# Sample-token products of several weight pairs run together, in a hybrid decoder step on one core

## The chip, the cores and the metric

The kernel runs on one core of one Trainium2 chip, as one launch. The metric is the device time of that launch in microseconds (us). The engines are named as the profile names them: PE (TensorE's matmuls) and PEld (its weight loads), DVE (VectorE), ACT (ScalarE), POOL (GpSimd) and SP (SyncE, which here issues most DMAs).

## The reference, cut to what matters

One layer of a decoder step for 1024 prompt tokens and 32 sample tokens (8 sequences of 4). Every token is normalised and modulated to `h`, `h` is projected by one wide matrix, an mLSTM branch and a windowed attention branch use the parts, two gates weigh the two output projections, and a last matrix ends the layer.

```python
def layer(x, c, C0, n0, m0, k_past, v_past, ...):
    h, gate = adaln_in(x, c, w_ada, b_ada, g_norm)
    (mq, mk, mv, mi, mf, mo, mz, aq, ak, av, az, gm, ga) = split_in(h @ w_in)
    y_m, C, n, m = mlstm_branch(mq, mk, mv, mi, mf, mo, mz, C0, n0, m0, ...)
    ...
    y_a = o.astype(x.dtype) * jax.nn.silu(az)
    u = jax.nn.sigmoid(gm) * (y_m @ w_mo) + jax.nn.sigmoid(ga) * (y_a @ w_ao)
    x = x + gate * (u @ w_o)
```

Both the prompt tokens and the sample tokens go through `h @ w_in`, `y_a @ w_ao` and so on, with the same weights.

## The kernel before, in words

**Products.** Each float32 operand is split into a high and a low part (`wh`, `wl` for weights; names ending in `h` and `l` for activations), and a product is made of three matmuls. ACT makes the high part by a cast, DVE the low part by a subtraction.

**Pairs.** 36 blocks of 128 output columns of `w_in` are done two at a time, as 18 pairs (class `Pair`, numbered 0 to 17): 0 to 3 belong to the mLSTM heads (`head_in`), 4 to 11 are the gates `ga` and `gm` (`gate`), 12 and 13 `az` (`query_gate`), 14 to 17 `mo` and `mz` (`head_gate`). A pair's prompt tokens are computed by seven block products in place of eight (a Strassen-like scheme): products 1 to 7 use sums and differences of four weight tiles, which DVE makes in place (`first_sums`, `split`). `block_products` runs them in the order 5, 6, 2, 7, then product 1 of the next pair, then 3, 4. Each product is 12 matmuls of 128x512 into the PSUM banks `bx`, `bw`, `by`, `bz`. Four pairs of `w_ao` (class `AttPair`, generator `att_products`, banks `ax`, `aw`, `ay`, `az`) follow the same way with half as many matmuls in a product; their operands `ya...` are made from `yr` tiles by ACT, DVE and POOL.

**Samples.** The 32 sample columns of a pair are not in these products. `samples` multiplies the raw weights with the sample tokens (`c32`) in a run of its own: 16 float32 matmuls (8 in the attention output) that use 32 columns of the array each, so that four work side by side, into a PSUM tile `smp` (`smpa`), which ACT copies to `smps`. One pair later `samples_end` transposes `smps` on PE into `smpo` (`halves_sum`, through `tr`), DVE adds the halves, and the pair's own function applies the gate to the samples (`gts`). In `block_products` both stand behind product 2 of pair n: first the transpose of pair n, then the sample run of pair n+1. In `att_products` they stand at the same place.

**Weights.** A pair's four raw tiles are loaded by SP (`nxt.load()` at product 5 of the pair before, two products ahead of the sample run) into a ring of nine tiles (`raw_tile`). Most other transient data, DMA targets included, live in 50 tiles of 128x512 (`ht`, tag "half").

**Order.** PE's order is the program's: `in_order` chains every matmul behind the last. On the other engines a scheduler orders the instructions when the kernel is built; `no_sync` gives it an order without a wait. `side` is a clock that the build keeps (`side.now`), by which other streams of work (the heads, the output weights) are set between the matmuls. SP issues its DMAs in one order, each waits at the head of the queue.

Of the kernel before, what the change touches and what calls it, by code (L numbers as in the profile page):

```python
# [15 lines left out]
ALU = mybir.AluOpType  # L16
# [8 lines left out]
NS = NB * NT  # L25
# [159 lines left out]
def body(tc, a):  # L185
    nc = tc.nc
    with ExitStack() as ctx:
# [35 lines left out]
        class Ordered:  # L223
            def __init__(self, eng, name):
                self.eng, self.name, self.on, self.late, self.before = eng, name, True, False, None

            def __getattr__(self, op):
                f = getattr(self.eng, op)

                def call(*args, **kw):  # L230
                    ins = f(*args, **kw)  # L231
                    i = getattr(ins, "ins", ins)
                    if self.on:
                        in_order(ins, self.name)
                    elif self.late and self.before is not None:
                        no_sync(i, [self.before])
                    self.before = i
                    return ins
                return call

        @contextmanager
        def not_before(*engs):
            for e in engs:
                e.late = True
            yield
            for e in engs:
                e.late = False

        V, S, G = Ordered(nc.vector, "V"), Ordered(nc.scalar, "S"), Ordered(nc.gpsimd, "G")
# [305 lines left out]
        def split_weights(raws, name, eng):  # L555
            parts = [split4(raw, f"{name}_{i}", eng) for i, raw in enumerate(raws)]
            return tuple((lambda k, w=w: w[k // 4][:, k % 4]) for w in zip(*parts))
# [3 lines left out]
        def piece(w, rh, rl, kn, name, p, evac):  # L561
            wh, wl = w
            c0, n = PIECES[p]
            banks.append(banks.pop(0))
            acc = banks[-1]([128, 384], f"g_{name}{p}")
            o = acc[:, :n]
            for k in range(kn):
                mm(o, wh(k), rh(k, c0, n), start=(k == 0), stop=False)
                mm(o, wh(k), rl(k, c0, n), start=False, stop=False)
                mm(o, wl(k), rh(k, c0, n), start=False, stop=(k == kn - 1))  # L570
                if k < kn - 1:
                    side.tick()
            evac(p, acc, c0, n)
            side.tick()

        hs = {}

# [834 lines left out]

        def halves_sum(sums):
            o, t = pb([128, 2, 2, NS], "smpo"), sums[:, 0:2 * NS].rearrange("p (c s) -> p c s", c=2)
            tr(o.rearrange("p c h s -> p (c h s)"), sums, ident)
            V.tensor_reduce(t, o.rearrange("p c h s -> p c s h"), op=ALU.add, axis=AX.X)
            return t

        class Pair:
# [5 lines left out]

            def load(self):
                for c, n in enumerate(self.names):
                    for kh in range(2):
                        t = self.raw[c, kh] = raw_tile(f"wr_{n[0]}{n[1]}_{kh}")
                        dma(t, a["w1"][JOBS[n]][:, 4 * kh:4 * kh + 4])  # L1430

            def samples(self):
                acc = pb([128, 128], "smp")
                for k in range(4):
                    for j in range(4):
                        mm(acc[32 * j:32 * j + 32], c32[:, 4 * (j % 2) + k], self.raw[j // 2, j % 2][:, k],
                           start=(k == 0), stop=(k == 3), share=4)
                self.sums = ht([128, 128], "smps")
                S.copy(self.sums, acc)

            def samples_end(self):
                self.kind.samples(self, halves_sum(self.sums))

            def first_sums(self, behind=None):
                self.raw["s1"] = raw_tile("ws1")
                V.tensor_tensor(self.raw["s1"], self.raw[1, 0], self.raw[1, 1], op=ALU.add)
                if behind is not None:
                    no_sync(V.before, [behind])
                V.tensor_tensor(self.raw[1, 0], self.raw[0, 0], self.raw[1, 0], op=ALU.subtract)
                V.tensor_tensor(self.raw[0, 0], self.raw["s1"], self.raw[0, 0], op=ALU.subtract)  # L1450

            def split(self, i):
                r = self.raw
                t = {1: r[0, 0], 2: r[0, 1], 3: r[0, 1], 4: r[1, 1], 5: r.get("s1"), 6: r[0, 0], 7: r[1, 0]}[i]
                self.w[i] = split4(t, f"p{self.name}_{i}_")
                if i == 2:
                    V.tensor_tensor(r[0, 1], r[0, 1], r[0, 0], op=ALU.subtract)
# [88 lines left out]
        class head_gate:  # L1546
# [14 lines left out]
            def samples(self, o):  # L1561
# [6 lines left out]
                store(ymD[h][:, SEQ:T], t[:, 0])  # L1568

        def block_products(jobs, hook):  # L1570
            flat = [(0, 1)]
# [26 lines left out]
            for j, (n, i) in enumerate(flat):  # L1598
                job_ = jobs[n]
                nxt = jobs[n + 1] if n + 1 < len(jobs) else None  # L1600
                hook(n, i)
                if i == 3 and not nxt:
                    job_.samples_end()
                job_.kind.ahead(job_, i)
                if i == (5 if n else 6) and nxt:
                    nxt.load()
                split_ahead(j + 2)
# [17 lines left out]
                elif i == 2:  # L1625
                    job_.done(0, 0, X)
                    behind = job_.weighted if job_.kind is query_gate else None
                elif i == 5:
                    p5 = ht([128, 512], "p5")
                    S.copy(p5, Z)  # L1630
                elif i == 3:
                    job_.done(0, 1, p5, W)
                elif i == 4:
                    job_.done(1, 0, Y)
                if i == (7 if n else 5):
                    job_.done(1, 1, p5, Y)
                if i == (2 if n else 7) and nxt:
                    job_.samples_end()
                    nxt.samples()
                    side.free["b"] = side.now + HOLD["b"]  # L1640
# [3 lines left out]
                if i == 7 and nxt and nxt.kind not in (head_in, gate):  # L1644
                    nxt.first_sums(behind)
                if j == 0 or (i == 3 and nxt):
# [49 lines left out]

        class AttPair:
            HOMES = {1: ("A", 0), 5: ("A", 2), 6: ("B", 0), 2: ("B", 2), 7: ("C", 0), 3: ("C", 2), 4: ("D", 0)}

            def __init__(self, i):  # L1700
                self.i, self.w, self.g = i, {}, {}

            def load(self):
                self.raw = [raw_tile(f"wr_ao{2 * self.i + c}") for c in range(2)]
                for c in range(2):
# [10 lines left out]

            def samples(self):
                acc = pb([128, 128], "smpa")
                for k in range(2):
                    for j in range(4):  # L1720
                        mm(acc[32 * j:32 * j + 32], c32[:, 2 * (j % 2) + k], self.raw[j // 2][:, 2 * (j % 2) + k],
                           start=(k == 0), stop=(k == 1), share=4)
                self.sums = ht([128, 128], "smps")
                S.copy(self.sums, acc)

            def samples_end(self):
                us = ut[self.i % 2][:, self.i // 2 * 2:self.i // 2 * 2 + 2, SEQ:T]
                V.scalar_tensor_tensor(us, self.ts, 1.0, halves_sum(self.sums), op0=ALU.add, op1=ALU.mult)

            def first_sums(self):  # L1730
                (r0, r1), s = self.raw, raw_tile("ws1")
                V.tensor_tensor(s[:, 0:2], r1[:, 0:2], r1[:, 2:4], op=ALU.add)
                V.tensor_tensor(r1[:, 0:2], r0[:, 0:2], r1[:, 0:2], op=ALU.subtract)
# [3 lines left out]
            def split(self, i):  # L1737
# [5 lines left out]
                hi, lo = self.w[i] = [x[:, o:o + 2] for x in self.g[home]]  # L1743
                S.copy(hi, t)
                V.tensor_tensor(lo, t, hi.bitcast(F32), op=ALU.subtract)
# [9 lines left out]
        def att_products():  # L1755
            jobs = [AttPair(i) for i in range(4)]
            flat = [(0, 1)]
# [17 lines left out]
            jobs[0].split(1)  # L1775
            jobs[0].samples()
            jobs[0].first_sums()
# [4 lines left out]
            for j, (n, i) in enumerate(flat):  # L1782
                job_ = jobs[n]
                nxt = jobs[n + 1] if n < 3 else None
                if i == 1 and nxt:
                    nxt.load()
                if i == 6:
                    if nxt:
                        nxt.gates()
                    if n in (0, 1, 3):  # L1790
# [282 lines left out]
        def hook(n, i):  # L2073
# [19 lines left out]
        work = block_products(pairs, hook)  # L2093
        att = att_products()
        side.add("g", ada_gate())
# [350 lines left out]
```

## Time and profile before

| | |
|---|---|
| median of 3 runs | 816.8 us (816.77 to 817.11) |
| the profiled execution's own time | 816.58 us |
| its span, first to last instruction | 814.8 us |
| mean granted TensorE clock | 0.995 |
| busy, share of the span | PE 98%, PEld 82%, DVE 74%, ACT 52%, POOL 10% |

Matmul records overlap since the engine is pipelined, so what a matmul costs is read here from start to start. In a timeline row the first number is the start in us from the span's start, the second the length, then engine, line, operation, output and inputs, shapes, and in brackets the idle time ahead with what ended it. An instruction of float32 in the sample runs leaves two records, so a run of 16 matmuls stands as x32 and one of 8 as x16. L286 and L291 are the helpers that record matmuls and transposes, L231 the one for DVE, ACT and POOL, L272 the one for DMAs.

### The profile page before, as it was taken

To read this page: it belongs to the slowest core of one execution; us is meant where nothing else is said; L and a number is where in the kernel's file an instruction comes from. 1 tells how busy PE (TensorE), PEld (TensorE's weight loads), DVE (VectorE), ACT (ScalarE), POOL (GpSimd) and SP (SyncE) were. 2 spreads that over 40 slices of the span, in tenths; PEclk is the share of its full clock that TensorE was granted. 3 is DMA by queue.
4 is the path that set the end of the run, shared out by engine and by line. 5 is a ranking of instruction groups with operands and counts; after the bars stand their busy time and mean duration, and the time that the engine had idled before them with its cause. 6 is when DMAs were issued, how large, how long until landed. Compare 5 with 4: busy or idle time off the path is not lost. (4 is left out here: it accounts for less than half of the span.)

```text
span 814.8 us, 15188 instructions
## 1 busy us (share of the span) xinstructions
PE 801.4 (98%) x5162; PEld 666.8 (82%) x5162; DVE 599.8 (74%) x1506; ACT 420.4 (52%) x1025; POOL 77.6 (10%) x156
## 2 busy tenths in 40 slices
PE   8999999999999999999999999999999999999996
PEld 5779888888788888888888888888888779997775
DVE  4899896755755557476668889898668997876666
ACT  5664356656565564546656555554446652224335
POOL 0120000010000000000001323231002101000000
PEclk9999999999999999999999999999999999999998
DMA  9994746646545424537764785864436589648622
GB/s 353 364 351 140 230 152 225 176 149 213 183 143 164 125 89 162 162 135 240 256 215 138 251 253 190 284 209 145 146 106 211 190 308 385 222 148 292 207 105 110
DMA packets 113218, 165.51 MB, mean 203 GB/s; under 512 B 21184, under 2 KB 55360, under 8 KB 113108
## 3 DMA queue, kind: packets, MB, share of 16 engines
q1 hardware_dynamic: 106740, 152.21, 56.2%
q10 hardware_dynamic: 4752, 7.60, 2.5%
q0 software_dynamic: 1648, 4.72, 1.5%
q8 instruction: 41, 0.67, 0.3%
q14 instruction: 37, 0.30, 0.1%
HBM read 115.51 MB, written 50.00 MB: 203 GB/s over the span
## 5 line engine op out<-in xcount | busy, mean ns | idle before, releaser
L231 ACT ACTIVATE p<-p,nmx 128x256 f32<-128x256 f32 (+1 forms) x64 | 31.1, 486 | 23.3 <-DVE nmx L231 23.2
L231 DVE CUSTOM_DVE_ANT_0 p<-sc,cst,sink 128x256 f32<-128x256 f32 (+1 forms) x64 | 26.1, 463 | 11.9 <-PE sc L286 11.8
L286 PE MATMUL g_aq<-h_h,wh_aq 128*128 128x384 f32 (+1 forms) x96 | 32.2, 336 | 0.0
L231 POOL TENSOR_SCALAR Cs<-Cs,sxb 128x129 f32<-128x129 f32 x32 | 27.6, 878 | 42.9 <-PE sn L286 42.9
L286 PE MATMUL g_aq<-h_h,wl_aq 128*128 128x384 f32 (+1 forms) x96 | 30.9, 322 | 0.0
L286 PE MATMUL g_aq<-h_l,wh_aq 128*128 128x384 f32 (+1 forms) x96 | 30.8, 321 | 0.0
L286 PE MATMUL g_w_mo<-ym_l,wh_w_mo 128*128 128x384 f32 (+1 forms) x96 | 30.8, 321 | 0.0
L286 PE MATMUL g_w_mo<-ym_h,wh_w_mo 128*128 128x384 f32 (+1 forms) x96 | 30.8, 321 | 0.0
L286 PE MATMUL g_w_mo<-ym_l,wl_w_mo 128*128 128x384 f32 (+1 forms) x96 | 30.8, 321 | 0.0
L272 POOL DMA_DIRECT2D oD<-uqv x16 | 8.7, 541 | 167.6 <-ACT uqv L231 167.6
L231 DVE COPY p<-pt 128x512 f32<-128x512 f32 (+1 forms) x16 | 10.5, 656 | 16.2 <-PE pt L291 16.2
L231 ACT CAST wosh<-wor 128x512 fp32r<-128x512 f32 x24 | 14.8, 621 | 13.8 <-DVE wor L231 13.0
L286 PEld LDWEIGHTS g_aq<-h_h,wh_aq 128*128 128x128 f32 x96 | 18.0, 188 | 2.5 <-issue 2.3
L231 DVE TENSOR_TENSOR wosl<-wor,wosh 128x512 fp32r<-128x512 f32 x24 | 16.5, 687 | 3.4 <-ACT wosh L231 3.2
L231 DVE SCALAR_TENSOR_TENSOR tgw_mo<-tgw_mo,g_w_mo 128x384 f32<-128x384 f32 (+1 forms) x24 | 12.4, 518 | 8.6 <-PE g_w_mo L286 6.8
L286 PE MATMUL g_mq<-h_h,wh_mq 128*128 128x384 f32 (+1 forms) x48 | 16.7, 348 | 1.6 <-ACT aq L231 1.2
L231 ACT ACTIVATE p<-p,den 128x256 f32<-128x256 f32 (+1 forms) x32 | 14.3, 490 | 7.6 <-DVE den L231 7.6
L286 PEld LDWEIGHTS g_aq<-h_l,wh_aq 128*128 128x128 f32 x96 | 18.1, 188 | 0.0
L286 PEld LDWEIGHTS g_w_mo<-ym_l,wh_w_mo 128*128 128x128 f32 x96 | 18.0, 188 | 0.0
L286 PEld LDWEIGHTS g_w_mo<-ym_h,wh_w_mo 128*128 128x128 f32 x96 | 18.0, 188 | 0.0
L286 PEld LDWEIGHTS g_w_mo<-ym_l,wl_w_mo 128*128 128x128 f32 x96 | 18.0, 188 | 0.0
L286 PEld LDWEIGHTS g_aq<-h_h,wl_aq 128*128 128x128 f32 x96 | 18.0, 188 | 0.0
(2068 smaller groups left out, 2827.6 us busy)
## 6 DMA issues: line engine op xcount, KB each, us to landing
early_h<-w_ada SPq DMA_DIRECT2D x8, 512.0 KB
adar_ga<-w_ada SPq DMA_DIRECT2D x16, 256.0 KB
wr_ga<-w SPq DMA_DIRECT2D x16, 256.0 KB
wr_gm<-w SPq DMA_DIRECT2D x16, 256.0 KB
taD<-gt SPq DMA_DIRECT2D x16, 256.0 KB
tmD<-gt SPq DMA_DIRECT2D x16, 256.0 KB
wor<-w_out SPq DMA_DIRECT2D x16, 256.0 KB
tga<-taD SPq DMA_DIRECT2D x16, 256.0 KB
```

Source lines behind the costliest of these rows:

```text
L231: ins = f(*args, **kw)
L272: ins = (eng or nc.sync).dma_start(out, in_)
L286: in_order(nc.tensor.matmul(out, lhsT, rhs, start=start, stop=stop, skip_group_check=more))
```

## The change

Two pairs' sample products are made in one run, and four in the attention output.

- `TOGETHER` names the pairs n = 4, 6, 8, 10, 12, 14. Behind product 2 of such a pair `nxt.samples(jobs[n + 2])` multiplies the samples of pairs n+1 and n+2 into one PSUM tile of 256 columns; one ACT copy takes it out. Behind product 2 of pair n+1 no sample run stands. `samples_end` of the first of the two transposes both (two transposes in a row) and adds the halves of both by one DVE instruction; the second of the two finds its part ready.
- For this, pair n+2 is loaded at product 1 of pair n, into the ring of nine tiles for n = 6, 10, 14 and into tiles of the 50 (`spare`) for n = 4, 8, 12.
- The attention output multiplies the samples of all its four pairs in the first run, into 512 columns, and transposes all four in a row. Its pairs 1 to 3 are loaded into `spare` tiles during pair 16.
- `behind` and `landed` give the scheduler orders without waits: the first cast and the first sum of weights that are now there earlier, and the second pair's gate on the samples, are set behind the matmul at which they stood before. A cast of the `mk` weights is set behind the last evacuation in the same way.
- `side.now` is advanced as if each pair's samples were still done at its old place.

```diff
-        def halves_sum(sums):
-            o, t = pb([128, 2, 2, NS], "smpo"), sums[:, 0:2 * NS].rearrange("p (c s) -> p c s", c=2)
-            tr(o.rearrange("p c h s -> p (c h s)"), sums, ident)
+        def halves_sum(sums, n=1):
+            o, t = pb([128, 2 * n, 2, NS], "smpo"), sums[:, 0:2 * n * NS].rearrange("p (c s) -> p c s", s=NS)
+            for g in range(n):
+                tr(o[:, 2 * g:2 * g + 2].rearrange("p c h s -> p (c h s)"), sums[:, 128 * g:128 * g + 128], ident)
             V.tensor_reduce(t, o.rearrange("p c h s -> p c s h"), op=ALU.add, axis=AX.X)
-            return t
+            return [t[:, 2 * g:2 * g + 2] for g in range(n)]
...
+            def samples(self, *more):
+                pairs_ = (self,) + more
+                acc = pb([128, 128 * len(pairs_)], "smp")
+                for g, p in enumerate(pairs_):
+                    p.first, p.was = self, side.now
+                    for k in range(4):
+                        for j in range(4):
+                            mm(acc[32 * j:32 * j + 32, 128 * g:128 * g + 128], c32[:, 4 * (j % 2) + k], p.raw[j // 2, j % 2][:, k],
+                               start=(k == 0), stop=(k == 3), share=4)
+                    p.cost = side.now - p.was
+                side.now = self.was + self.cost
+                self.sums = ht([128, 128 * len(pairs_)], "smps")
                 S.copy(self.sums, acc)
...
+        TOGETHER = {4: False, 6: True, 8: False, 10: True, 12: False, 14: True}
+        spare = lambda name: ht([128, 512], name).rearrange("p (k e) -> p k e", e=128)
...
+                if i == 6 and n - 1 in TOGETHER:
+                    nxt.landed = [last["PE"]]
+                if i == 1 and n in TOGETHER:
+                    jobs[n + 2].load(raw_tile if TOGETHER[n] else spare)
...
                 if i == (5 if n else 6) and nxt:
-                    nxt.load()
+                    if n in TOGETHER:
+                        nxt.load()
+                    elif n - 1 not in TOGETHER:
+                        nxt.load()
...
                 if i == (2 if n else 7) and nxt:
                     job_.samples_end()
-                    nxt.samples()
+                    if n in TOGETHER:
+                        nxt.samples(jobs[n + 2])
+                    elif n - 1 in TOGETHER:
+                        side.now += nxt.cost
+                    else:
+                        nxt.samples()
...
-            jobs[0].samples()
+            jobs[0].samples(jobs)
...
                     if nxt:
                         job_.samples_end()
-                        nxt.samples()
+                        side.now += nxt.cost
...
+                if i == 3:
+                    for p in att_pairs[1:]:
+                        p.load(spare)
```

What this does to the order of instructions is shown at three places. On PE, behind product 2 of pair 5 (`bx` is its bank), where the transpose of pair 5 and the sample run of pair 6 stood, before:

```order
L286 MATMUL bx<-h_l_603,wh_pgate_2__4287 128x512
L286 MATMUL bx<-h_h_602,wl_pgate_2__4288 128x512
L291 MATMUL smpo<-cst,smps 128x128
L286 MATMUL smp<-wr_ga_0_4279,c_102 32x128
L286 MATMUL smp<-wr_ga_1_4281,c_102 32x128
L286 MATMUL smp<-wr_gm_0_4283,c_102 32x128
L286 MATMUL smp<-wr_gm_1_4285,c_102 32x128
```

and now:

```order
L293 MATMUL bx<-h_l_603,wh_pgate_2__4303 128x512
L293 MATMUL bx<-h_h_602,wl_pgate_2__4304 128x512
L298 MATMUL smpo<-cst,smps 128x128 x2
L293 MATMUL by<-t3h_887,wh_pgate_7__4333 128x512
L293 MATMUL by<-t3l_888,wh_pgate_7__4333 128x512
```

The 16 sample matmuls of pair 6 have moved to the run of pair 5, some 24 us earlier, and the two transposes are left. Nothing else moved on PE: apart from sample runs and transposes its rows are the same in the same order.

On DVE, late in pair 16 and early in pair 17 (`hg` and `hg1z` are gate evacuations, `wl_phead_gate` low parts of weights, `yr` differences for the attention operands, `wr_mo` and `ws` sums of weights), before:

```order
L231 SCALAR_TENSOR_TENSOR hg_7462<-hg_7462,hg1z 128x512
L231 TENSOR_TENSOR yr<-yr 128x512
L231 TENSOR_TENSOR wl_phead_gate_6__7517<-wr_mo_0_7341,wh_phead_gate_6__7516 128x512
L231 TENSOR_TENSOR yr<-yr 128x512
L231 TENSOR_TENSOR hg_7508<-p_7367,bw 128x512
L231 TENSOR_TENSOR wl_phead_gate_2__7545<-wr_mo_1_7343,wh_phead_gate_2__7544 128x512
L231 TENSOR_TENSOR wr_mo_1_7343<-wr_mo_1_7343,wr_mo_0_7341 128x512
L231 SCALAR_TENSOR_TENSOR hg_7462<-hg_7508,hg_7462 128x512
L231 TENSOR_TENSOR ws_7860<-wr_ao_7758 128x256
L231 TENSOR_TENSOR hg_7462<-hg_7462,ho 128x512
```

and now:

```order
L231 SCALAR_TENSOR_TENSOR hg_7432<-hg_7432,hg1z 128x512
L231 TENSOR_TENSOR wl_phead_gate_6__7499<-wr_mo_0_7314,wh_phead_gate_6__7498 128x512
L231 TENSOR_TENSOR hg_7490<-p_7340,bw 128x512
L231 TENSOR_TENSOR yr<-yr 128x512
L231 TENSOR_TENSOR wl_phead_gate_2__7527<-wr_mo_1_7316,wh_phead_gate_2__7526 128x512
L231 SCALAR_TENSOR_TENSOR hg_7432<-hg_7490,hg_7432 128x512
L231 TENSOR_TENSOR wr_mo_1_7316<-wr_mo_1_7316,wr_mo_0_7314 128x512
L231 TENSOR_TENSOR hg_7432<-hg_7432,ho 128x512
L231 SCALAR_TENSOR_TENSOR hg_7519<-hg_7519,by 128x512
L231 TENSOR_TENSOR wl_phead_gate_7__7571<-wr_mz_0_7318,wh_phead_gate_7__7570 128x512
L231 SCALAR_TENSOR_TENSOR hg_7519<-hg_7381,hg_7519 128x512
L231 TENSOR_TENSOR yr<-yr 128x512
```

The two `yr` differences now stand behind the evacuation that reads `bw`, and the first sum `ws` of the second attention pair has gone from here to where that pair begins.

On SP, around the loads of pair 5 (`hq` to `qw` are a head's next group of data; the numbers 4014 and 4022 are pair 5, 3895 pair 6), before:

```order
L272 DMA wr_gm_1_3708<-w 128x512
L272 DMA hq_2_3913<-qD_140 128x256
L272 DMA hk_2_3914<-kD_141 128x256
L272 DMA hv_2_3915<-vD_142 128x256
L272 DMA et<-nmd 128x256
L272 DMA qw<-wid 128x256
L272 DMA wr_ga_0_4014<-w 128x512
```

and now:

```order
L279 DMA wr_gm_1_3708<-w 128x512
L279 DMA wr_ga_0_3895<-w 128x512
L279 DMA wr_ga_1_3897<-w 128x512
L279 DMA wr_gm_0_3899<-w 128x512
L279 DMA wr_gm_1_3901<-w 128x512
L279 DMA hq_2_3921<-qD_140 128x256
L279 DMA hk_2_3922<-kD_141 128x256
L279 DMA hv_2_3923<-vD_142 128x256
L279 DMA et<-nmd 128x256
L279 DMA qw<-wid 128x256
L279 DMA wr_ga_0_4022<-w 128x512
```

The four loads of pair 6 have come ahead of the head's five. In the same way six loads of attention weights (`wr_ao`) now stand between the first and the last three of the four small loads that fill `c32` for the attention output.

More of the change, by code (lines that the diff above doesn't have):

```diff
@@ L224, in __init__ @@
             def __init__(self, eng, name):
-                self.eng, self.name, self.on, self.late, self.before = eng, name, True, False, None
+                self.eng, self.name, self.on, self.late, self.before, self.behind = eng, name, True, False, None, []
             def __getattr__(self, op):
@@ L555, in split_weights @@
         def split_weights(raws, name, eng):
-            parts = [split4(raw, f"{name}_{i}", eng) for i, raw in enumerate(raws)]
+            with behind(S, emptied if name[:2] == "mk" else []):
+                parts = [split4(raw, f"{name}_{i}", eng) for i, raw in enumerate(raws)]
             return tuple((lambda k, w=w: w[k // 4][:, k % 4]) for w in zip(*parts))
@@ L1424, in __init__, with load @@
                 self.raw, self.w, self.held = {}, {}, {}
-            def load(self):
+            landed = ()
+            def load(self, tile=raw_tile):
                 for c, n in enumerate(self.names):
                     for kh in range(2):
-                        t = self.raw[c, kh] = raw_tile(f"wr_{n[0]}{n[1]}_{kh}")
+                        t = self.raw[c, kh] = tile(f"wr_{n[0]}{n[1]}_{kh}")
                         dma(t, a["w1"][JOBS[n]][:, 4 * kh:4 * kh + 4])
[L1432 to L1438, printed above, removed]
+            def samples(self, *more):
[10 more added lines that the diff above has]
+                self.sums = ht([128, 128 * len(pairs_)], "smps")
@@ L1439, in samples @@
                 S.copy(self.sums, acc)
             def samples_end(self):
-                self.kind.samples(self, halves_sum(self.sums))
-            def first_sums(self, behind=None):
+                f = self.first
+                if f is self:
+                    n = self.sums.shape[1] // 128
+                    was = side.now
+                    self.sums = halves_sum(self.sums, n)
+                    side.now = was
+                side.now += 0.11
+                now = [] if f is self else [last["PE"]]
@@ L1445, in first_sums @@
+                with behind(S, now), behind(V, now):
+                    self.kind.samples(self, f.sums.pop(0))
+            def first_sums(self, others=()):
                 self.raw["s1"] = raw_tile("ws1")
-                V.tensor_tensor(self.raw["s1"], self.raw[1, 0], self.raw[1, 1], op=ALU.add)
-                if behind is not None:
-                    no_sync(V.before, [behind])
+                with behind(V, [*others, *self.landed]):
+                    V.tensor_tensor(self.raw["s1"], self.raw[1, 0], self.raw[1, 1], op=ALU.add)
@@ L1701, in __init__, with load @@
                 self.i, self.w, self.g = i, {}, {}
-            def load(self):
-                self.raw = [raw_tile(f"wr_ao{2 * self.i + c}") for c in range(2)]
+            def load(self, tile=raw_tile):
+                self.raw = [tile(f"wr_ao{2 * self.i + c}") for c in range(2)]
                 for c in range(2):
@@ L1715, in gates, with samples @@
                     dma(self.ts[:, c], taD[2 * self.i + c][:, SEQ:T])
[L1717 to L1724, printed above, removed]
-            def samples_end(self):
+            def samples(self, jobs):
+                acc = pb([128, 4, 128], "smpa")
+                for g, p in enumerate(jobs):
+                    was = side.now
+                    for k in range(2):
+                        for j in range(4):
+                            mm(acc[32 * j:32 * j + 32, g], c32[:, 2 * (j % 2) + k], p.raw[j // 2][:, 2 * (j % 2) + k],
+                               start=(k == 0), stop=(k == 1), share=4)
+                    p.first, p.cost = self, side.now - was
+                    if g:
+                        side.now = was
+                self.sums = ht([128, 512], "smps")
+                S.copy(self.sums, acc.rearrange("p g e -> p (g e)"))
+            def samples_end(self):
+                if self.first is self:
+                    was = side.now
+                    self.sums = halves_sum(self.sums, 4)
+                    side.now = was
+                side.now += 0.11
                 us = ut[self.i % 2][:, self.i // 2 * 2:self.i // 2 * 2 + 2, SEQ:T]
-                V.scalar_tensor_tensor(us, self.ts, 1.0, halves_sum(self.sums), op0=ALU.add, op1=ALU.mult)
+                with behind(V, [last["PE"]] if self.i else []):
+                    V.scalar_tensor_tensor(us, self.ts, 1.0, self.first.sums.pop(0), op0=ALU.add, op1=ALU.mult)
             def first_sums(self):
                 (r0, r1), s = self.raw, raw_tile("ws1")
-                V.tensor_tensor(s[:, 0:2], r1[:, 0:2], r1[:, 2:4], op=ALU.add)
+                with behind(V, self.landed):
+                    V.tensor_tensor(s[:, 0:2], r1[:, 0:2], r1[:, 2:4], op=ALU.add)
                 V.tensor_tensor(r1[:, 0:2], r0[:, 0:2], r1[:, 0:2], op=ALU.subtract)
@@ L1743, in split @@
                 hi, lo = self.w[i] = [x[:, o:o + 2] for x in self.g[home]]
-                S.copy(hi, t)
+                with behind(S, self.landed if i == 1 else []):
+                    S.copy(hi, t)
                 V.tensor_tensor(lo, t, hi.bitcast(F32), op=ALU.subtract)
@@ L1755, in att_products @@
         def att_products():
-            jobs = [AttPair(i) for i in range(4)]
+            jobs = att_pairs
             flat = [(0, 1)]
@@ L2093, in body @@
         work = block_products(pairs, hook)
+        att_pairs = [AttPair(i) for i in range(4)]
         att = att_products()
```

20 lines of the change are left out of this document (14 added, 6 removed).

## The prediction

> **What bounds the kernel now.** I read the page's busy times and its 40 slices first, then what ended PE's waits, then PE's timeline around a sample run.
>
> ```profile
> PE 801.4 (98%) x5162; PEld 666.8 (82%) x5162; DVE 599.8 (74%) x1506; ACT 420.4 (52%) x1025; POOL 77.6 (10%) x156
> PE   8999999999999999999999999999999999999996
> DVE  4899896755755557476668889898668997876666
> PE g_mq L286 <- ACT aq L231: 1.2, 1, 1.2
> PE aw L286 <- ACT aw L231: 0.5, 1, 0.5
> ```
>
> PE is full from the first slice to the last; no other engine is, over the whole. The two waits (total, count, longest) are among the few that PE has. So time is won only by taking PE instructions out or making them denser, or by ending one of the waits, and it is lost if another engine comes late. A sample run lies on PE's own path: what it takes is the time from the start of the block matmul ahead of it to the start of the one behind it, less the steps of the block matmuls.
>
> ```profile
> 355.61 0.39 PE L286 MATMUL bx<-h_h,wl_pgate__4288 128*128 128x512 f32 x1
> 355.85 0.27 PE L291 MATMUL smpo<-cst,smps 128*128 128x128 f32 x1
> 356.05 0.30 PE L286 MATMUL smp<-wr_ga,c 128*32 128x128 f32 x2
> 356.18 0.28 PE L286 MATMUL smp<-wr_ga,c 128*32 128x128 f32 x2
> 356.83 0.28 PE L286 MATMUL smp<-wr_ga,c 128*32 128x128 f32 x2
> 357.06 0.50 PE L286 MATMUL by<-t3h,wh_pgate__4317 128*128 128x512 f32 x1
> 357.39 0.39 PE L286 MATMUL by<-t3l,wh_pgate__4317 128*128 128x512 f32 x1
> 359.69 0.39 PE L286 MATMUL by<-t3h,wl_pgate__4318 128*128 128x512 f32 x1
> ```
>
> A block matmul steps by 0.23 (357.39 to 359.69 is 2.30 in ten steps). From the last `bx` to the second `by` is 1.78, two steps of which would be there anyway: transpose, run and the way back into full tiles cost 1.32. Inside the run, four records side by side step by 0.108 (356.18 to 356.83, six steps), so the run's 32 records are 8 groups, 0.87. The other 0.45 is the transpose and the change of tile shape at both ends. Only this fixed part can be saved.
>
> **The change part by part: PE.** Three prices are still wanted: a transposition with no run behind it, a further one, and an entry with no transposition ahead.
>
> ```profile
> 673.38 0.39 PE L286 MATMUL aw<-yat2h,wl_ao3B 128*128 128x512 f32 x1
> 673.61 0.27 PE L291 MATMUL smpo<-cst,smps 128*128 128x128 f32 x1
> 673.64 0.47 PE L286 MATMUL ax<-yab21h,wh_ao3B 128*128 128x512 f32 x1
> 673.95 0.39 PE L286 MATMUL ax<-yab21l,wh_ao3B 128*128 128x512 f32 x1
> 118.61 1.03 PE L291 MATMUL pt<-cst,p 128*128 128x128 f32 x8
> 119.41 0.38 PE L286 MATMUL g_aq<-h_h,wh_aq 128*128 128x288 f32 x1
> 630.21 0.39 PE L286 MATMUL by<-t3h,wl_phead_gate__7589 128*128 128x512 f32 x1
> 630.52 0.64 PE L286 MATMUL smpa<-wr_ao,c 128*32 128x128 f32 x16
> 643.19 0.39 PE L286 MATMUL ax<-yab21h,wl_ao0B 128*128 128x512 f32 x1
> 644.53 0.39 PE L286 MATMUL ay<-yat3l,wh_ao0C 128*128 128x512 f32 x1
> 522.43 1.08 PE L286 MATMUL smp<-wr_az,c 128*32 128x128 f32 x32
> 523.33 0.40 PE L286 MATMUL sn<-Cs,qd 128*32 128x129 f32 x8
> ```
>
> A lone transposition: 673.38 to 673.95 is 0.57, less two steps, 0.11. A further one: eight in 0.80 (118.61 to 119.41), 0.10. An entry without one: 0.31 from `by` to `smpa` (630.21 to 630.52) against 0.44 from `bx` to `smp` (355.61 to 356.05), so a run that loses its transposition is 0.12 shorter.
>
> - Pairs 5 and 6: the run behind pair 4 gets 8 more groups, +0.87; behind pair 5 the 1.32 goes, and two transpositions stay, 0.11 + 0.10. Together -0.24.
> - Pairs 7/8, 9/10, 11/12 and 15/16 have the same, and their run has no transposition ahead any more (the run before took it): -0.24 - 0.12 = -0.36 each, -1.44.
> - Pairs 13/14: the run of 522.43 is followed by `sn`, which uses tiles of 32 columns too and comes after 0.90, just the 8 groups. There is no way back to save. I take 0.
> - Pair 17: its run stays alone and loses its transposition, -0.12.
>
> The pairs give -1.80. In the attention output a pair's run is 4 groups (x16 records). The first run gets 12 more, +1.30. The run in the second place takes 1.34 less two steps, 0.88 (643.19 to 644.53); four transpositions stay of it, 0.11 + 3 x 0.10, so -0.47. The runs in the third and fourth place go, -0.88 each, and the lone transposition of 673.61, -0.11. Sum -1.04; on PE, -2.84 in all. By this reading a run keeps its 0.108 whatever its length.
>
> **A wait that I expect to shrink.** The 0.5 at `aw`:
>
> ```profile
> 639.49 0.39 PE L286 MATMUL az<-ym_l,wl_ao0A 128*128 128x512 f32 x1
> 640.34 0.50 PE L286 MATMUL aw<-yat2h,wh_ao0B 128*128 128x512 f32 x1 [0.47 <-ACT aw L231]
> 638.09 0.40 ACT L231 CAST wh_ao1A<-wr_ao 128x256 fp32r<-128x256 f32 x1
> 638.40 0.40 ACT L231 CAST wh_ao1A<-ws 128x256 fp32r<-128x256 f32 x1
> 639.70 0.59 ACT L231 COPY aw<-ax 128x512 f32<-128x512 f32 x1
> ```
>
> From `az` to `aw` is 0.85, 0.62 over a step. PE waits for a copy that stands behind two casts for the second attention pair, 0.31 each. In the new order on ACT those casts come after the copy, and PE gets here 1.30 later because of the longer first run, with the copy's own inputs no later than PE makes them. The copy reads what PE made (`ax`), so part of its lateness moves with PE. Between 0 and -0.62 I take -0.5, near the upper end, since the casts' 0.61 alone covers the wait.
>
> **What DVE may give back.** The attention stage is DVE's:
>
> ```profile
> 630.00:680.00 50.00, 49.53 (x271) 39.15 (x270) 46.28 (x104) 29.86 (x69) 7.39 (x6) 1.00 0.79 273
> 614.87 0.69 DVE L231 TENSOR_TENSOR yr<-yr 128x512 f32<-128x512 f32 x1 [1.19 <-POOL yab22l L231]
> 652.04 0.42 DVE L231 TENSOR_TENSOR wl_ao1B<-wr_ao,wh_ao1B 128x256 fp32r<-128x256 f32 x1
> L286 PE MATMUL aw<-yat2h,wl_ao1B x2: 393/395/397, 651.8 to 652.5; 128*128 128x512 f32 x2
> ```
>
> The window's columns are length, then the busy times of PE, PEld, DVE, ACT and POOL, the clock (1.00), the DMA share and GB/s: DVE works 46.28 of 50. The low part `wl_ao1B` ends at 652.46; PE's matmul with it, the second of the tile's two, starts near 652.5. That margin is about nothing. The two `yr` differences of 0.69 stood in a stretch where DVE had 1.19 idle; now they come behind the evacuation of `bw`, in the full stretch: up to +1.38, and the longer add of the halves +0.13. Against it, PE asks 1.30 later from the first attention run on, and three small adds leave the stage. Between 0 and +1.5 I take +0.4, nearer zero because 1.30 of the 1.5 is covered by PE's own delay, until the later runs that are gone give that back to PE.
>
> **Costed at nothing.** The held cast of `mk`: PE's 1.2 at `g_mq` waits for `aq` and not for it. The halves' additions, gates and copies: fewer instructions on DVE and ACT in the pairs, where PE waits for neither. The casts and sums of early weights keep their places. POOL's order is unchanged. SP remains:
>
> ```profile
> 299.31 0.33 SPq L272 DMA_DIRECT2D hq<-qD  x1
> 302.81 0.44 PE L286 MATMUL oT<-p,ukv 128*64 128x128 f32 x4
> 321.12 0.42 DVE L231 TENSOR_TENSOR et<-et,cst 128x256 f32<-128x256 f32 x1
> 611.31 0.85 SPq L272 DMA_DIRECT2D c<-yaD  x2
> ```
>
> Four loads of pair 6 now stand ahead of `hq` and the rest of its head's group. One of their tiles is free only after the `oT` matmul, so `hq` goes from 299.31 to about 303.3 plus 4 x 0.33, and `et`, last in the group, is first used at 321.12: some 16 us cover it. Six attention loads now stand ahead of the last `c` loads of 611.31; at 0.33 to 0.45 each that is 2 to 2.7, and `smpa` reads `c` at 630.52, so 16 us of cover less the landing.
>
> **The sum.** The profiled execution took 816.58, 0.22 under the median. -2.84 - 0.5 + 0.4 = -2.94 gives 813.6 on it and 813.9 on the median.
>
> **Rivals.** 0.2% (1.6 us) is about what a measurement of this kernel can tell from no change: 815.2 and 818.4 are the bounds.
>
> *DVE becomes the bound of the attention stage.*
>
> ```profile
> 621.48 1.78 DVE L231 TENSOR_TENSOR wl_phead_gate__7589<-wr_mz,wh_phead_gate__7588 128x512 fp32r<-128x512 f32 x1
> 621.28 1.43 POOL L231 TENSOR_TENSOR yab21l<-yr,yab21h 128x512 fp32r<-128x512 f32 x1 [1.81 <-ACT yab21h L231]
> ```
>
> A DVE subtraction of two tiles that takes 0.69 elsewhere took 1.78 when it started 0.2 into a POOL instruction; it ended 0.55 after POOL's. The moved `yr` differences and the low parts around them now fall among POOL's three subtractions at 613 to 623, in another phase. One more collision adds 1.1, two 2.2; with the +0.4 kept and PE's 1.30 as cover only once, the time is 815.0 to 816.1. For it: the missing margin at `wl_ao1B`. Against it: most of 630 to 680 has no POOL work (7.39 us). [...]
>
> *The run doesn't close up.* If 8 more groups cost what the second run did apart from its transposition (1.32 - 0.12 = 1.20 instead of 0.87), the five gaining pairs lose 0.33 each and the attention's three lose about 0.33 each as well, together 2.64: 816.5. Against it: the even 0.108 within a run and 0.90 for a whole run ahead of `sn`.
>
> *Slower: SP stands at the attention loads.* A load into one of the 50 tiles waits until the tile's last reader is done, and everything behind it on SP waits too, the last `c` loads among it, without which the attention's one long sample run can't start, and PE with it. It decides once `c` lands after 630.5; to end beyond 818.4 it must be 4.5 late, at 635. With a tile that comes free 5 us too late, 818.9. For it: tiles of that pool are held by the attention operands, whose makers (DVE) are behind. Against it: the 16 us.
>
> **How the numbers follow.** The forecast's mechanism: 0.64, with an own range of 812.9 to 815.0 (DVE's +1.5 in place of 0.4 at the top; none of it and a full 0.62 at the bottom). Better than that: 0.05. DVE the bound: 0.15, two thirds of it above 815.2. Runs that don't close up: 0.06. SP: 0.10. Faster 0.64 + 0.05 + 0.05 = 0.74, same 0.10 + 0.06 = 0.16, slower 0.10. The range 812.9 to 816.2 leaves out the better case, SP, and the top of "same", about 0.2.
>
> **What would show it.** Right: from `bx` to the second `by` behind pair 5 near 0.67 in place of 1.78, the run behind pair 4 about 1.74 long in place of 0.87, the first attention run near 1.9, and no bracket at `aw`. Wrong: brackets on PE in the attention stage that name `wl_ao`, `yat` or `yab` (DVE or POOL), or one at `smpa` that names a DMA; sample groups stepping by more than 0.108; or block matmuls that start late behind a pair's product 5 for want of weights.

## The result, and the profile after

The change makes the kernel slower: 823.3 us (822.5 to 824.4, 5 runs) against 816.8 (816.3 to 817.1, 5 runs), a ratio of 1.008 with a 95% interval of 1.0069 to 1.0091. The forecast was 813.9, between 812.9 and 816.2, with 0.10 for slower.

PE's waits in the profile after (total, count, longest), with two lines of the page ahead. From here on the helpers that record matmuls, transposes and DMAs are L293, L298 and L279 in every kernel but before and the one with 48 tiles.

```profile
PE 804.1 (98%) x5162; PEld 670.5 (82%) x5162; DVE 598.4 (73%) x1497; ACT 419.8 (51%) x1016; POOL 79.1 (10%) x156
PEclk9999999999999999999999999999999999999999
PE stk L298 <- ACT hv L231: 1.9, 1, 1.9
PE smp L293 <- DMA wr_az<-w: 1.8, 3, 1.4
PE ax L293 <- DVE u_h L231: 1.3, 1, 1.3
```

PE's share is as before, and the slices show nothing at all: the loss is three short holes that before did not have. The prediction's saving is there too. PE's order apart from sample runs and transposes is the same in both, so I set the start of every other matmul in the two traces against each other; where the difference jumps, time was lost or won (each jump is taken from the settled difference ahead of the place to the settled one behind it):

| place (us of after) | difference jumps by | what it is |
|---|---|---|
| run behind pair 4, then behind 5 | +0.84, -1.08 | forecast -0.24 together |
| runs behind 6 and 7, 8 and 9 | +0.97, -1.10, +0.75, -1.10 | forecast -0.36 each two |
| 448.9 to 453 | +3.7 | `stk` waits, and what follows it |
| runs behind 10 and 11 | +0.75, -1.08 | forecast -0.36 |
| 524.6 to 531.8, run of 13 and 14 | +5.3, then -0.7 | forecast 0 together |
| runs behind 14 and 15, then behind 16 | +0.75, -1.13, then -0.12 | forecast -0.36, then -0.12 |
| attention: first run; `aw`; second place | +1.28, -0.76, -0.44 | forecast +1.30, -0.5, -0.47 |
| 653.9, `ax` of the second attention pair | +1.6 | waits for `u_h` |
| attention: third and fourth place | -0.88, -0.90 | forecast -0.88 each |
| 462.4 and 664, two small waits of `bx` and `ax` | +0.28, +0.26 | |

The first hole, on PE, and what ACT did ahead of it (`stk` is a transpose in a head's work, `hv` a copy on ACT):

```profile
446.63 0.40 PE L293 MATMUL bz<-h_h,wl_pgate__5372 128*128 128x512 f32 x1
448.90 0.44 PE L298 MATMUL stk<-cst,kvq 128*128 128x128 f32 x2 [1.88 <-ACT hv L231]
...
442.61 0.62 ACT L231 CAST wosh<-wor 128x512 fp32r<-128x512 f32 x1 [1.49 <-DMA yhD<-yt]
445.67 0.62 ACT L231 CAST wosh<-wor 128x512 fp32r<-128x512 f32 x1 [2.44 <-DMA yhD<-yt]
446.19 0.48 ACT L231 COPY et<-n 128x387 f32<-128x387 f32 x1
448.49 0.36 ACT L231 COPY hv<-tv 128x256 f32<-128x256 f32 x1
```

`wosh` casts output weights that are wanted much later. They stand 1.49 and 2.44 at the head of ACT's queue for a transfer of `yt`, which they do not read: it only empties the tile of 128x512 that the cast is to write. Behind them stand `et`, eight more instructions and `hv`, and for `hv` PE waits. The second hole starts on SP (with one row of DVE between):

```profile
513.41 0.47 SPq L279 DMA_DIRECT2D wr_az<-w  x1
...
521.00 0.55 DVE L231 TENSOR_TENSOR vm<-vf,vm 32x388 fp32r<-32x388 f32 x1
...
521.58 0.32 SPq L279 DMA_DIRECT2D ho<-oD  x1
521.95 1.38 SPq L279 DMA_DIRECT2D wr_az<-w  x3
```

The load of `ho` (a gate's operand, in one of the 50 tiles) stands from 513.9 to 521.6. In the kernel as built it waits for a DVE instruction on `vm`, the last user of its tile, which ended at 521.55 in the row shown. Three of the four weight loads of pair 13 stand behind it, and the sample run at 524.6 finds their tiles empty. Before, `ho` went out at once:

```profile
510.71 1.56 SPq L272 DMA_DIRECT2D wr_az<-w  x2
512.37 0.41 SPq L272 DMA_DIRECT2D ho<-oD  x1
```

Both places lie where four `spare` tiles are taken out of the 50 (pairs 10 and 14). And both holes cost more than they last. Windows of after around the first and the second hole (columns as in the prediction; the clock is the eighth number, ahead of the DMA share):

```profile
448.00:450.00 2.00, 1.10 (x6) 0.98 (x7) 0.25 (x2) 1.99 (x11) 0.93 (x7) 0.92 1.04 379
450.00:452.00 2.00, 2.00 (x6) 1.59 (x5) 1.71 (x6) 1.53 (x4) 0.17 (x3) 0.50 0.22 81
452.00:454.00 2.00, 2.00 (x8) 1.53 (x8) 1.94 (x5) 0.67 (x2) 0.00 (x0) 0.73 0.04 8
...
528.00:530.00 2.00, 2.00 (x40) 1.98 (x44) 1.86 (x4) 0.00 (x0) 0.00 (x0) 0.54 1.05 403
530.00:532.00 2.00, 2.00 (x45) 1.79 (x34) 0.83 (x2) 0.37 (x1) 0.36 (x1) 0.60 1.06 405
```

Taken as either 1.0 or 0.5, the granted clock is 0.5 for 3.4 us after each hole (0.32 + 2.0 + 1.08 of the three windows; 1.84 + 1.60 of the two), and by that some 1.7 us more are lost at each.

### The profile page after: what moved, and what is told of

Read it like the earlier page. It is cut to its first block, busy times and chain, and to the rows that moved or that the text cites. A ratio compares the mean times of both kernels' runs of the same rounds, so it can differ in the third digit from the quotient of the medians.

```text
span 821.5 us, 15162 instructions
## 1 busy us (share of the span) xinstructions
PE 804.1 (98%) x5162; PEld 670.5 (82%) x5162; DVE 598.4 (73%) x1497; ACT 419.8 (51%) x1016; POOL 79.1 (10%) x156
## 4 chain that ended last, share of the span: by engine, by line
PE 88%; DVE 5%; DMA 3%; ACT 2%; issue 1%; SPq 0%; POOL 0%; ACTq 0%; DVEq 0%; POOLq 0%
PE bx L293 11%; PE bw L293 11%; PE by L293 11%; PE bz L293 6%; PE g_w_mo L293 6%; PE g_aq L293 4%; PE g_mq L293 3%; PE foW L293 3%; PE foY L293 2%; PE foX L293 2%; PE smp L293 2%; PE sc L293 2%; PE oT L293 2%; PE pt L298 2%; PE n L293 1%; PE g_mk L293 1%
## 5 line engine op out<-in xcount | busy, mean ns | idle before, releaser
L293 PE MATMUL g_aq<-h_h,wh_aq 128*128 128x384 f32 (+1 forms) x96 | 32.2, 336 | 0.0
L293 PE MATMUL g_aq<-h_h,wl_aq 128*128 128x384 f32 (+1 forms) x96 | 30.9, 322 | 0.0
L293 PE MATMUL g_aq<-h_l,wh_aq 128*128 128x384 f32 (+1 forms) x96 | 30.8, 321 | 0.0
L293 PE MATMUL g_w_mo<-ym_l,wh_w_mo 128*128 128x384 f32 (+1 forms) x96 | 30.8, 321 | 0.0
L293 PE MATMUL g_w_mo<-ym_h,wh_w_mo 128*128 128x384 f32 (+1 forms) x96 | 30.8, 321 | 0.0
L293 PE MATMUL g_w_mo<-ym_l,wl_w_mo 128*128 128x384 f32 (+1 forms) x96 | 30.8, 321 | 0.0
L279 POOL DMA_DIRECT2D oD<-uqv x16 | 8.7, 542 | 167.7 <-ACT uqv L231 167.7
L293 PEld LDWEIGHTS g_aq<-h_h,wh_aq 128*128 128x128 f32 x96 | 18.0, 188 | 2.5 <-issue 2.3
L293 PE MATMUL g_mq<-h_h,wh_mq 128*128 128x384 f32 (+1 forms) x48 | 16.7, 348 | 1.5 <-ACT aq L231 1.2
L293 PEld LDWEIGHTS g_aq<-h_l,wh_aq 128*128 128x128 f32 x96 | 18.1, 188 | 0.0
L293 PEld LDWEIGHTS g_w_mo<-ym_l,wh_w_mo 128*128 128x128 f32 x96 | 18.0, 188 | 0.0
L293 PEld LDWEIGHTS g_w_mo<-ym_h,wh_w_mo 128*128 128x128 f32 x96 | 18.0, 188 | 0.0
L293 PEld LDWEIGHTS g_w_mo<-ym_l,wl_w_mo 128*128 128x128 f32 x96 | 18.0, 188 | 0.0
L293 PEld LDWEIGHTS g_aq<-h_h,wl_aq 128*128 128x128 f32 x96 | 18.0, 188 | 0.0
```

The lines of the kernel that those rows point to most:

```text
L279: ins = (eng or nc.sync).dma_start(out, in_)
L293: in_order(nc.tensor.matmul(out, lhsT, rhs, start=start, stop=stop, skip_group_check=more))
```

## The experiments

Each was compared with the kernel before on the same chip (medians of 816.26 to 816.44 there).

**Parts of the change.** The pairs without the attention, whose edits are all undone, as here:

```diff
-            jobs[0].samples(jobs)
+            jobs[0].samples()
...
-                        side.now += nxt.cost
+                        nxt.samples()
```

> The pairs' part of the change without the attention's. Theory of the tiles: the spare tiles of pairs 10 and 14 are taken out of the 50, a cast on ACT and a load on SP then wait for a tile at the head of their queues, and PE stands for what is behind them; two stalls of some 2 us, each followed by a stretch at half clock, 8.3 together as in the changed kernel, less 1.4 for the pairs: about +6.9, 823.7. Rival, the loss belongs to the attention stage or to both parts together: 815 to 816.

Measured 822.6 (ratio 1.006 to 1.0089): the loss is the pairs'. PE's waits are the two holes again:

```profile
PE smp L293 <- DMA wr_az<-w: 2.2, 1, 2.2
PE stk L298 <- ACT hv L231: 1.9, 1, 1.9
```

The early loads without any run put together:

```diff
-                    if n in TOGETHER:
-                        nxt.samples(jobs[n + 2])
-                    elif n - 1 in TOGETHER:
-                        side.now += nxt.cost
-                    else:
-                        nxt.samples()
+                    nxt.samples()
```

> All early loads of the pairs as in the changed kernel, spare tiles too, but every pair's samples in a run of their own at the old place; attention as before. Theory of the tiles: the stalls come without any run put together, about 816.8 + 8.3 = 825 (the one that ended with the late weights of pair 13 as well, since its run reads them at the same place). Rival, the long run is what waits: about 816.8.

Measured 823.8 (1.0076 to 1.0116), with both holes in the profile, the second one shorter:

```profile
PE stk L298 <- ACT hv L231: 2.0, 1, 2.0
PE smp L293 <- DMA wr_az<-w: 1.8, 2, 1.2
```

So the loads alone bring the loss; no run put together is needed for it. The profiled execution here took 821.8 and has no slow clock at the first hole, though that lasted 2.0:

```profile
450.00:452.00 2.00, 2.00 (x10) 1.68 (x10) 1.14 (x5) 1.96 (x6) 0.57 (x5) 1.00 0.58 222
```

The runs of this kernel go from 821.8 to 828.1, and the mean granted clock falls from 0.998 to 0.992 between them. I take it that a hole is followed by a slow stretch in some executions and not in others; the windows are those of the profiled one alone.

**No spare tiles.** Only three of the pairs of runs, with the ring of nine alone:

```diff
-        TOGETHER = {4: False, 6: True, 8: False, 10: True, 12: False, 14: True}
+        TOGETHER = {6: True, 10: True, 14: True}
```

> Only pairs 7/8, 11/12 and 15/16 are run together, whose early loads go into the ring of nine; no spare tile is taken, and the attention output is as before. Theory of the tiles: neither stall, and three times the saving of 0.25 to 0.36, so 815.7 to 816.1. Rival, the loads ahead on SP's queue or the long run itself cost: a stall behind pairs 8, 12 or 16, over 817.

Measured 828.3 (1.0134 to 1.0167). The tiles' side of this was badly set: in the changed kernel the ring has room for pair n+2 because the pair before it sits in spare tiles. Without them, as the program is built, the ring itself is short; no row names the tile that is waited for, but the last load of pair 11 leaves SP only at 483.68, and the weights land late:

```profile
PE smp L293 <- DMA wr_gm<-w: 8.8, 2, 6.5
```

It says nothing for or against the 50 tiles, only that four more tiles have to come from somewhere. The test of the 50 is the kernel before with two tiles fewer:

```diff
-            return sp.tile(shape, dt, tag="half", bufs=50, name=name)
+            return sp.tile(shape, dt, tag="half", bufs=48, name=name)
```

> The kernel before with 48 tiles of 128x512 in place of 50 and nothing else. Theory of the tiles: ACT and SP stand for tiles at some places, and PE behind them, some us slower, 818 to 825. If there were tiles to spare: 816.3.

Measured 824.8 (1.0081 to 1.0122): nothing else was changed in the program, and PE gets a hole of 3.2 at another place:

```profile
PE bw L286 <- ACT bw L231: 3.2, 1, 3.2
```

So the pool of 50 has no two tiles to spare. How this hole comes about isn't shown: with 48 tiles the build also orders ACT's work otherwise there. The first two pairs of runs alone:

```diff
+        TOGETHER = {4: False, 6: True}
```

> Only pairs 5/6 and 7/8 are run together (spare tiles once, at pair 6, then the ring); all else as before. By the prediction's prices -0.24 - 0.36 - 0.12 = -0.7, 815.5, since no stall was seen at those pairs. If any four tiles taken out cost something: 816.3 or more.

Measured 816.55 (0.9988 to 1.0005): by its median the second case, but the interval still holds the -0.7 of the first. Behind pairs 4 and 5 all is as forecast (+0.84, -1.08), but the run of pairs 7 and 8 took 1.35 more instead of 0.75: its weights came late there too, by little, and the runs go from 815.5 to 817.1.

**Each hole closed by order alone.** First `ho`, set on SP behind the four weight loads of pair 13 (the call that issues it also moves behind them in the program; apart from `ho` SP's order stays as it was):

```diff
+                        behind_load.extend(free[-4:] if n == 12 else [])
...
             dma(o, src[:, HALF[th]])
+            no_sync(free[-1], behind_load)
```

> The pairs' part alone, with one order added: the load of ho at pair 12 stands on SP behind the four weight loads of pair 13 and not among them. If the stall at pair 13's samples is SP standing at the head of its queue for ho's tile, it goes: 822.6 less 4.4 (what the stall and the slow stretch took in that profile beyond the 0.87 of eight groups), 818.2; the stall at stk stays. If the weights of pair 13 were late for another reason (too much on the DMA engines), 822 to 823.

Measured 818.5 (1.0017 to 1.0036), with no wait left at pair 13's samples. SP still stands for the tile until 521.3, and nobody minds:

```profile
513.58 2.58 SPq L279 DMA_DIRECT2D wr_az<-w  x4
521.33 0.33 SPq L279 DMA_DIRECT2D ho<-oD  x1
```

With one stage of the output weights' casts 5 us later besides:

```diff
                 keep("b22", k, b22)
-                yield lag, ""
+                yield lag + (5.0 if k == KA[1] else 0.0), ""
```

> The run with ho behind the weights, and one stage of the output weights (casts of wosh on ACT) 5 us later on the build's clock, so that no cast gets a tile that a transfer of yt still holds. If the stall at stk is ACT standing for that tile, it goes with the 0.65 behind it: 818.5 - 2.4 = 816.1. If hv was late for its own inputs, the stall stays: 818 to 819.

Measured 816.45 (0.9989 to 1.0006, 815.2 to 817.7). The hole is gone; ACT's row for `hv` and PE's for `stk`:

```profile
444.31 0.37 ACT L231 COPY hv<-tv 128x256 f32<-128x256 f32 x1
446.43 0.38 PE L298 MATMUL stk<-cst,kvq 128*128 128x128 f32 x2
```

What remains is 0.7 at `bx`. PE waits there for a gate's evacuation on ACT (`gt`, at 458.12), ahead of which ACT now does the samples' gate `gts`, for which it waits 1.52 for DVE, and two casts; before, `gts` came behind it:

```profile
PE bx L293 <- ACT gt L231: 0.7, 1, 0.7
```

Next the weights of pair 7, which in the runs so far went out behind a head's `et` and `qw`, and these stood (for tiles, as the program is built). In the run with `ho` behind the weights the run of 7 and 8 took 2.15 more instead of 0.75:

```profile
367.43 0.42 SPq L279 DMA_DIRECT2D tmD<-gt  x1
369.92 0.32 SPq L279 DMA_DIRECT2D et<-nmd  x1
370.95 0.32 SPq L279 DMA_DIRECT2D qw<-wid  x1
371.32 0.90 SPq L279 DMA_DIRECT2D wr_ga<-w  x2
```

```diff
+                if (n, i) == (5, 4):
+                    jobs[7].load()
...
                     if n in TOGETHER:
-                        nxt.load()
+                        if n != 6:
+                            nxt.load()
```

> As the run with later casts, and the four loads of pair 7 on SP ahead of the head's group that waits for tiles of pair 6. If the +1.3 to +2.1 at the run of pairs 7 and 8 (0.75 expected) is SP standing for those tiles, then all of the pairs' -1.8 is there: 814.6 to 815.2. If the weights come late for the traffic: 816.

Measured 815.9 (0.9984 to 1.0002, 815.2 to 817.0): that is nearer to 816, and a gain over the run with later casts isn't shown, whose runs lie between 815.2 and 817.7. In its profile the run of 7 and 8 takes the 0.75, but so it does in the profile of the run with later casts, where these loads went out later than in the rows above:

```profile
372.01 0.93 SPq L279 DMA_DIRECT2D wr_ga<-w  x2
372.98 2.03 SPq L279 DMA_DIRECT2D wr_gm<-w  x2
```

So SP's order alone doesn't decide whether these weights come late; how long their transfers take may, and that stays open. In the profile, of 815.85, all of the pairs' saving is there, less the 0.7 at `bx` and 0.2 at the second attention pair.

**The attention output.** Alone, with the pairs as before, their edits undone:

```diff
-        TOGETHER = {4: False, 6: True, 8: False, 10: True, 12: False, 14: True}
+        TOGETHER = {}
```

> Only the attention output's four runs are put together, the pairs are as before. From the changed kernel, in which this stage gained nothing: 816.8 within 0.4, with a wait of about 1.4 at the first block of the second attention pair, for DVE. By the prediction's sum (if that wait came only from the lateness that the pairs left behind): 815.3 to 815.8.

Measured 816.17 (0.9988 to 1.0005): no gain, with the wait that the changed kernel has:

```profile
PE ax L293 <- DVE u_h L231: 1.3, 1, 1.3
```

So it isn't a lateness that the pairs leave behind. In the new order on DVE the sums of the second pair's weights, the first of which `landed` sets behind a matmul of product 6, come ahead of `u_h` (two rows of after); before, the last two of them came behind it (two rows of before):

```profile
652.51 0.42 DVE L231 TENSOR_TENSOR wr_ao<-ws,wr_ao 128x256 f32<-128x256 f32 x1
653.19 0.68 DVE L231 SCALAR_TENSOR_TENSOR u_h<-tga,ax 128x512 f32<-128x512 f32 x1
644.51 0.68 DVE L231 SCALAR_TENSOR_TENSOR u_h<-tga,ax 128x512 f32<-128x512 f32 x1
645.78 0.41 DVE L231 TENSOR_TENSOR wr_ao<-ws,wr_ao 128x256 f32<-128x256 f32 x1
```

All of them set behind it:

```diff
-                with behind(V, self.landed):
+                with behind(V, [*self.landed, V.before] if self.i else []):
```

> The attention's four runs put together, as in the run of that alone (816.2), with the first sums of the next attention pair's weights set behind the evacuation of its product 2 on DVE, where they stood in the kernel before. If the wait for DVE at the second attention pair is that order, 1.47 less: 814.7 to 815.2. If DVE is simply full there (46 of 50 us), the wait comes back at another place: 816.0 to 816.3.

Measured 816.12 (0.9986 to 1.0004). The wait came back at other places, in pieces:

```profile
PE az L293 <- DVE wl_ao1A L231: 0.4, 1, 0.4
PE ax L293 <- DVE u_h L231: 0.2, 1, 0.2
```

By matmul starts 1.5 of the 1.6 is lost again (+0.48 at `ax`, +1.03 up to the next `aw`). DVE is full there: 23.96 of 24 us in the changed kernel (this row), and 23.73 before.

```profile
640.00:664.00 24.00, 22.69 (x101) 17.84 (x99) 23.96 (x53) 14.65 (x34) 3.80 (x2) 1.00 0.50 159
```

**All together, in order.** The whole change with the three orders of the pairs and the attention's:

> The whole change with these three orders and the attention's sums behind the evacuation. The pairs' -1.8 as in the run without the attention, and from the attention nothing, since DVE sets its end: 814.5 to 815.2. If the attention's wait was only its late start: 813.5 to 814.

Measured 815.06 (ratio 0.9972 to 0.999; 814.8 to 816.3): the version that beats both. The profile has the whole saving of the runs, the 0.7 at `bx`, and 0.4 from the attention (the difference goes from -1.23 ahead of the stage to -1.62 behind it; in the run with the sums moved back alone it went from 0.33 to -0.05).

## Why the prediction was wrong, point by point

- **PE's prices held.** A pair of transpositions with no run behind it takes 0.68 from `bx` to the second `by`, where 0.67 was forecast; the run behind pair 8, 64 records, goes from its first to its last in 1.68, 0.108 a group; and the first attention run takes 1.89 up to the transposition, where 1.9 was forecast:

```profile
356.16 0.39 PE L293 MATMUL bx<-h_h,wl_pgate__4304 128*128 128x512 f32 x1
356.39 0.38 PE L298 MATMUL smpo<-cst,smps 128*128 128x128 f32 x2
356.52 0.48 PE L293 MATMUL by<-t3h,wh_pgate__4333 128*128 128x512 f32 x1
356.84 0.39 PE L293 MATMUL by<-t3l,wh_pgate__4333 128*128 128x512 f32 x1
637.19 1.96 PE L293 MATMUL smpa<-wr_ao,c 128*32 128x128 f32 x64
639.08 0.33 PE L298 MATMUL smpo<-cst,smps 128*128 128x128 f32 x1
```

  In the run with later casts, where no run waits for weights, the six runs put together give -0.24, -0.35, -0.35, -0.33, +0.02 and -0.38, and pair 17 -0.12: -1.75 against -1.80. The rival of runs that don't close up is out.
- **The step that failed is "costed at nothing": what the spare tiles cost SP and ACT.** For the pairs it priced one of the three places where spare tiles are taken (pair 6), and there what the four loads put ahead of `hq` on the queue, some 16 us of cover. It did not ask who else takes tiles out of the 50, and what stands behind those on their queues. Two of the three places had no cover: +3.7 and +4.5 (5.3 less the 0.75 that such a run takes). At pair 6 the run of 7 and 8 lost between nothing and 1.4 in the profiles; its weights stood behind `et` and `qw` on SP, but what made them late in some runs and not in others is open. The sentence on the slower rival had the mechanism (SP stands for a tile, and what is behind it waits), but put it at the attention's loads alone, where no wait came, and left out ACT, whose two casts waited for tiles in the same way (1.49 and 2.44).
- **The slow clock was in no term.** The profile before has one such stretch while PE works, in its first 12 us, behind a wait of 1.4 for `xc` (its windows are in the last section), so a hole that brings half clock could have been seen there. No row of before shows when a hole does so.
- **The range.** By its own terms (816.8 - 2.84 - 0.62) the bottom is 813.3, not 812.9.
- **Attention.** `aw` gave -0.76 (forecast -0.5, at most -0.62), the runs about what was said, and DVE took 1.6 + 0.3 back (forecast 0.4, bound 1.5). The named rival, DVE the bound of this stage, came true in its place and, at 1.9, in its size, but not by its cause: from 605 us on before, and in the same work after, five instructions of DVE run longer than others of their kind and shape beside one of POOL in each trace, by 3.7 us in sum before and 3.7 after. DVE is simply full, in whatever order the sums stand. The rival stood beside the forecast with 0.15, on a row of 46.28 of 50 us that said it plainly.

## What to carry to other kernels

Ask of every tile that a change holds longer: which pool is it from, who takes the next one, and what stands behind that instruction on its engine's queue. At the two holes here a load moved ahead cost by the tiles that it held: orders on SP and ACT closed them, with the same loads. Where an engine is busy 46 of 50 us in a stage, ask what work that another engine is spared there can be worth: here it was 0.4 of the 1.04 forecast on PE. And where time is lost in short holes, the page's slices don't show it, but the start of each matmul set against the kernel before does.

## What the runs showed of the hardware

The hole of 1.9 us on PE at `stk` cost 3.7: the granted clock then fell to 0.50. It did so for 3.4 us after the holes of 1.9 and 1.8 (in three waits) of after, and for two such lengths at the 3.2 of the kernel with 48 tiles, where block matmuls start 0.43 apart (300.38 to 300.81) in place of 0.23 and these windows sum to 1.68 + 2 + 2 + 1.16 = 6.8:

```profile
298.00:300.00 2.00, 1.06 (x3) 0.87 (x4) 1.97 (x5) 1.59 (x3) 0.00 (x0) 0.58 0.34 131
300.00:302.00 2.00, 2.00 (x6) 1.61 (x5) 0.70 (x2) 0.58 (x1) 0.00 (x0) 0.50 0.38 143
302.00:304.00 2.00, 2.00 (x6) 1.52 (x5) 0.00 (x0) 0.00 (x0) 0.00 (x0) 0.50 0.00 0
304.00:306.00 2.00, 2.00 (x13) 1.90 (x13) 0.69 (x1) 1.96 (x6) 0.00 (x0) 0.71 0.00 0
```

After 2.0 at `stk` (the loads alone), 1.6 there (`ho` behind the weights) and 1.3 (the attention of after) it did not fall: the windows from 450 to 456 in those two and from 640 to 664 in after are at 1.00. So the length of a hole alone doesn't say whether the clock falls after it, and no run shows what does. In the kernel before it fell once while PE worked, for the same length (0.12 + 2.0 + 1.28: the window from 6 to 8, at 0.97, and the two below), about 1 us after a wait of 1.4 at the start:

```profile
8.00:10.00 2.00, 2.00 (x12) 0.62 (x12) 1.77 (x4) 1.22 (x3) 0.00 (x0) 0.50 1.05 392
10.00:12.00 2.00, 1.96 (x11) 0.48 (x4) 1.56 (x4) 0.00 (x1) 0.00 (x0) 0.68 1.05 396
```
